# Expert groups of one 64-token and two 32-token experts in place of groups of four, in a fused attention and mixture-of-experts block

## The chip, the cores and the metric

The kernel runs on one core of one Trainium2 chip. The metric is device time in microseconds (us) of one execution. In the texts PE is TensorE, DVE is VectorE, ACT is ScalarE, POOL is GpSimd and SP is SyncE, whose queue issues nearly all transfers.

## The reference, cut to what matters

The block has one layer: RMS norm, one input projection, two groups of attention heads, an output projection into the residual stream, RMS norm, and a mixture of experts. There are 512 tokens of 1024 features. The change lies in the last part:

```python
pg = softmax(hf @ wg + bg); gsel = argmax(pg)                 # one of 4 expert groups per token
le = (hf @ we + be).reshape(n, 4, 8)[gsel]                    # its 8 experts
p_top, e_loc = top_k(softmax(le), 2)                          # two experts per token
gate = pg_sel * p_top / sum(p_top)
ys = (silu(xb @ w1[e]) * (xb @ w3[e])) @ w2[e]                # for each of 32 experts, on its own tokens
out[token] += gate * ys                                       # w1, w3: 1024 x 512, w2: 512 x 1024, float32
```

The 32 experts together hold 192 MB (1 MB here is 2^20 bytes, the size of one tile), so the weights of each expert are six tiles of [128, 2048] float32, two halves h of w1, of w3 and of w2, and 192 tiles are loaded in all.

## The kernel before, in words

**Up to about 280 us** the kernel runs the projections and the attention, and then the router. It leaves `pr`, with the count and the running position of each token in each expert.

**Order of the experts.** `sort_experts` (L1078) and `name_experts` (L1089) bring the 32 experts into an order of *places*: the first FIXED = 4 places are the experts 0 to 3, whatever their counts, and the places behind are the other experts by falling count. So the weights of the fixed places can be loaded before the router is done, and those of the others only when `who_i`, the list of names, is written. For them SP reads the name into a register (`values_load`) and the transfer's address depends on it. The last 12 places (from SMALL = 20 on) get 32 slots for tokens, the others 64. Tokens beyond that are the business of `overflow` (L1329), a branch that isn't taken here but whose condition every engine reads; it lies in group PAUSE = 7.

**Groups.** The experts are worked off in 13 groups (L657): ten pairs of 64-slot experts, and three groups of four 32-slot experts, at the places 20, 24 and 28, as groups 2, 7 and 12. A group always fills the 128 columns of PE: the tokens of expert e stand in the columns `d["parts"][e]`, 64 or 32 wide, and the products of the experts of a group (L1222 for w1 and w3, L1278 for w2) go to different columns of PE, and to different partitions of one accumulator in PSUM. They are issued expert by expert within each step r.

**Work of one group**: `hidden` (L1225) goes through four parts, each of four steps r and of one tile per expert: w1h0, w1h1, w3h0, w3h1 (group 0: w1h0, w3h0, w1h1, w3h1). Behind each of the 16 steps it issues what the lists `during` (L1413) hold for that step: for the group before, the eight sums `combine` (L1317: two products, L1325 and L1326, and an addition on DVE, L1327), and for the group behind, the gathering of its tokens by products with a one-hot matrix (`quarter`, L1164, and `turn`). The one-hot matrix is one comparison on DVE (`match`, L914). Then `turn_hidden` turns the result (L1261), and `outputs` (L1288) does the products with w2, in two halves. The first `combine` writes the sums into the tile `ma`, once the weights in it aren't needed any more.

**The ring.** The weight tiles go into places that are listed in `slots` (L662) and are taken in turn by `ring_tile` (L669): 19 places the first time, 17 afterwards, as the two places of `ma` then hold the sums. A transfer waits on SP's queue until the last product that read the old tile in its place is done, and everything behind it on that queue waits too. The order of a group's loads is part by part, and within a part expert by expert (`load_parts`, L691). Loads of group 1 that don't depend on the sort (8 of 12 tiles) are issued ahead of group 0's work, by calls of `next(ahead)` (L990, L1051). At most eight loads are in flight at a time.

**Around the branch**: of group 8 only the first tile is requested ahead of the branch in group 7 (L1411), and the rest behind it, at step 7 of the hidden products (L1430).

Of the kernel before, what the change touches and what calls it, by code (L numbers as in the profile page):

```python
# [3 lines left out]

# [1 line left out]

# [5 lines left out]
F32 = mybir.dt.float32  # L12
F32R = mybir.dt.float32r
# [9 lines left out]
P = 128  # L23
SEQ = 512
D = 1024
NT = SEQ // P
# [1 line left out]
NE = 32  # L28
HID = 512
SLOTS = 64  # L30
FIXED = 4
SMALL = 20
EPS = 1e-6
BIG = 1e30
# [60 lines left out]
def tile_block(ctx: ExitStack, tc: tile.TileContext, a: dict, out: bass.AP):  # L95
# [550 lines left out]
    for i, (g, n, j) in enumerate(ORDER):  # L646
# [7 lines left out]
    NP = NE // 2  # L654


    groups = [(0, 2), (2, 2), (20, 4), (4, 2), (6, 2), (8, 2), (10, 2), (24, 4), (12, 2), (14, 2), (16, 2), (18, 2),  # L657
              (28, 4)]
    NG = len(groups)
    pools = {"w8": pool_w8, "q8": pool_q8, "mx": pool_mx}  # L660
    ring, both = [0], []
    slots = [("q8", tag, 2) for tag in ("bt", "qs", "kl", "kh")] + [("xs", "e0", 1), ("xs", "e1", 1)]  # L662
    slots += [("q8", tag, 2) for tag in ("qs", "kl", "kh")] + [("n", "n0", 1), ("n", "n1", 1)]
    slots += [("mx", "ma", 1), ("mx", "ma", 1), ("mx", "mb", 2)]
    slots += [("w8", tag, 2) for tag in ("w_h", "w_l", "w_h", "w_l")]
    slots += [("mx", "mb", 2)]
    slots[0] = ("q8", "bt", 1)

    def ring_tile():  # L669

        pool, tag, bufs = slots[ring[0] % len(slots)]
        ring[0] += 1
        if tag == "ma":
            if ring[0] > len(slots):
                return ring_tile()
            if not both:
                both.append(pools[pool].tile([P, 2, 2048], F32, tag=tag, name=tag, bufs=bufs))
                return both[0][:, 0]
            return both[0][:, 1]
        return pools[pool].tile([P, 2048], F32, tag=tag, name=tag, bufs=bufs)  # L680
# [9 lines left out]

    def load_parts(i):  # L691
        last = i == NG - 1
        first, n_exp = groups[i]
        if first < FIXED:
            who = [first + e for e in range(n_exp)]
        else:
            who = [nc.values_load(place_id[0][0:1, first + e:first + e + 1], engines=[mybir.EngineType.SP],
                                  min_val=0, max_val=NE - 1) for e in range(n_exp)]
        t = {}
        for n, h in hidden_order(i) + [("w2", 0), ("w2", 1)]:  # L700
            src = {"w1": w1, "w3": w3, "w2": w2}[n]
            cuts = (0, 1024, 2048) if last and n + str(h) in ("w31", "w20") else (0, 2048)
            if last and n + str(h) == "w21":
                cuts = (0, 1024, 1536, 2048)
            for c, m in zip(cuts, cuts[1:]):
                for e in range(n_exp):
                    if (i, n, h, e) == (0, "w2", 1, 1):
                        continue
                    if c == 0:
                        t[n, h, e] = ring_tile()  # L710
                    dst, part = t[n, h, e], expert(who[e], h)(src)
                    if first >= FIXED:
                        part = part.rearrange("o p f -> p (o f)")
                    nc.sync.dma_start(dst[:, c:m], part[:, c:m])
                    if m == 2048:
                        yield t
        yield t
# [6 lines left out]

    place_id = []
    loads, ahead = load_parts(0), load_parts(1)


    x_tile = []
# [181 lines left out]
        ts_ = slice(t, t + 2)  # L911
        nc.vector.scalar_tensor_tensor(rank[:, ts_], pr[:, ts_], 1.0, act[:, ts_], op0=ALU.add, op1=ALU.mult)

    def match(oh, rk, ts_):  # L914
        n = ts_.stop - ts_.start
        m, w = oh.shape[2:]
        nc.vector.tensor_tensor(oh[:, ts_], rk[:, ts_].unsqueeze(3).to_broadcast([P, n, m, w]),
                                iota_s[:, :w].unsqueeze(1).unsqueeze(1).to_broadcast([P, n, m, w]), op=ALU.is_equal)

    def gather_part(px, oh, h, ts_):  # L920

        for t in ts_:
            x2 = x_tile[0][:, t, h * 512:(h + 1) * 512].rearrange("p (r b) -> p r b", r=4)
            one = oh[:, t].rearrange("p e s -> p (e s)").bitcast(F32)
            for r in range(4):
                nc.tensor.matmul(px[h][:, r], lhsT=x2[:, r], rhs=one, start=(t == NT - 1 and r == 0),
                                 stop=(t == 0 and r == 3), skip_group_check=True)
# [59 lines left out]
    next(loads), next(loads)  # L987
    while (1, 0) not in mixed:
        wv.step()
    next(ahead)  # L990
    wv.fill(3)
    xs = x_tile[0]
    while wv.step():
# [15 lines left out]
    entries = book[:, P:P + NT * 6 * NP].rearrange("p (t q c) -> p t q c", t=NT, q=NP)  # L1009
    pr = bank("o", (P, NT + 1, NE))  # L1010
    rank = small([P, NT, NE], "rank")
    oh0 = pools["n"].tile([P, NT, 2, SLOTS], F32R, tag="oh", name="oh", bufs=1)
    def half_match(n, t):
        for _ in range(n):
            yield
        place(t)
        match(oh0, rank[:, :, 0:2], slice(t, t + 2))

    def gates_first():
        for _ in range(10):  # L1020
# [26 lines left out]
    for s in range(NT):  # L1047
        nc.tensor.matmul(pr[:, NT], lhsT=ones_b, rhs=act[:, s], start=(s == 0), stop=(s == NT - 1))
    gather_part(px, oh0, 1, (2,))
    for _ in range(7):  # L1050
        next(ahead)  # L1051
    run(half_match(0, 0))
    nc.vector.reduce_sum(gs, ge, axis=AX.X)
# [67 lines left out]
    def wk(tag, shape, dt=F32, bufs=1):  # L1121
        return work.tile(list(shape), dt, tag=tag, name=tag, bufs=bufs)

    def one_hot(rk, second=False):
        n = rk.shape[-1]
        shape = [P, NT, n, P // n]
        if second:
            oh = wk("oht", shape, F32R, bufs=2)
        else:
            oh = pools["n"].tile(shape, F32R, tag="oh", name="oh", bufs=1)  # L1130
        match(oh, rk, slice(0, NT))
        return oh

    def dispatch(oh, p, px=None):

        ohs = [oh[:, t].rearrange("p e s -> p (e s)") for t in range(NT)]
        n_exp, w_exp = oh.shape[2:]
        rows = [slice(w_exp * e, w_exp * e + w_exp) for e in range(n_exp)]  # L1140
        d = {"px": px, "parts": rows}

        spare = not isinstance(p, int)

        def gather(h, ts_=tuple(reversed(range(NT)))):
            if not d["px"]:
# [40 lines left out]
        def finish(tag="mm"):  # L1187
            pbs = [bank(tag, (P, 2, 2, P)) for _ in range(2)]
            for t in range(NT):
                pb = pbs[t // 2][:, t % 2]  # L1190
                if not spare:
                    both = bass.AP(tensor=book.tensor, offset=book.offset,
                                   ap=[book.ap[0], [P + t * 6 * NP, 2], [1, P]])
                    nc.tensor.matmul(pb, lhsT=ohs[t], rhs=both, start=True, stop=True)
                else:
                    nc.tensor.matmul(pb[:, 0], lhsT=ohs[t], rhs=book[:, :P], start=True, stop=True)
                    nc.tensor.matmul(pb[:, 1, :6], lhsT=ohs[t], rhs=p[:, t], start=True, stop=True)
                yield
            oht = wk("st", [P, NT, P], F32R) if spare else wk("oht", [P, NT, P], F32R, bufs=2)
            own, bufs = ("x", 1) if spare else ("", 2)  # L1200
            gsl = pools["n"].tile([P, 1], F32, tag="gsl" + own, name="gsl", bufs=bufs)
            rsl = pools["n"].tile([P, 1], F32, tag="rsl" + own, name="rsl", bufs=bufs)
            m = 3 * n_exp
            g4 = pools["n"].tile([P, NT, 12], F32, tag="g4" + own, name="g4", bufs=bufs)
            c = 0 if spare else 6 * p
            for u, pb in enumerate(pbs):
                nc.scalar.copy(oht[:, 2 * u:2 * u + 2], pb[:, :, 0])
                nc.vector.tensor_copy(g4[:, 2 * u:2 * u + 2, :m], pb[:, :, 1, c:c + m])
            for e, part in enumerate(rows):
                x = 6 * (e // 2) + 2 * (e % 2)  # L1210
# [118 lines left out]
    def overflow():  # L1329
# [12 lines left out]
        with tc.If(rounds > 0):  # L1342
            move(rank_s[:, :, SMALL:], SLOTS // 2)
            with tc.For_i(0, rounds, 1):
                move(rank_s, -SLOTS)
                with tc.For_i(0, NP, 1) as iv:
# [5 lines left out]
                    dd = dispatch(one_hot(rk), own)  # L1352
# [27 lines left out]
            move(rank_s[:, :, SMALL:], -SLOTS // 2)  # L1380

    def group_dispatch(i, oh=None, px=None):
        first, n = groups[i]
        if oh is None:
            oh = one_hot((rank if first < FIXED else rank_s)[:, :, first:first + n], i == 1)
        return dispatch(oh, first // 2, px)

    d = group_dispatch(0, oh0, px)
    d["gather"](0, (1, 0))
# [15 lines left out]
    for i in range(NG):  # L1405
# [2 lines left out]
            rounds = nc.values_load(cint[0:1, 0:1], min_val=0, max_val=7)  # L1408
        if not last:
            rest = ahead if i == 0 else load_parts(i + 1)  # L1410
            for nxt in islice(rest, 1) if i == PAUSE else rest:  # L1411
                pass
        during, after = [[] for _ in range(16)], [[] for _ in range(8)]  # L1413
        if i == 0:
            def first_gather(d=d):
                d["gather"](1, (1, 0))
                d["take"](1)

            during[1] = [name_experts]
            during[3] = [turn_places]  # L1420
            during[4] = [first_gather]
            during[7] = [sort_places, partial(begin, 1)]
            during[11] = [lambda d=d: run(d["finish"]("o"))]
        else:
            for n in range(8):
                at_ = (3 if n < 4 else 7) if last else 3 + n // 2 if i == PAUSE else 4 + n // 2 * 2
                during[at_].append(partial(combine, *prev, n // 4, (n % 4,), i == 1))
        if not last:
            if i == PAUSE:
# [116 lines left out]
```

## Time and profile before

| | us |
|---|---|
| median of 3 runs (752.1 to 754.06) | 753.59 |
| the profiled execution | 753.97 |
| its span, from the first to the last instruction | 752.3 |
| PE busy | 726.8 (97%) |
| DVE busy | 389.1 (52%) |
| ACT busy | 302.2 (40%) |
| moved by DMA | 228.86 MB, mean 304 GB/s |

The page shows the span in 40 equal slices, so one slice is 18.8 us, and each digit is a busy share in tenths. A busy PE is not a PE at its peak, since products of several column ranges run at once and their ends are modelled. A row of a timeline gives the start and the length in us, the engine and the line, what is written and read, and in brackets the idle time before it with what ended it. A product of float32 leaves two records.

### The profile page before, as it was taken

What the parts mean: (1) busy time and instruction counts of PE and PEld (TensorE: products, weight loads), DVE (VectorE), ACT (ScalarE), POOL (GpSimd) and SP (SyncE); (2) the same over time, 40 slices, a digit from 0 to 9 for tenths busy, and PEclk for the clock granted to TensorE, in tenths of its full rate; (3) what the DMA queues carried; (4) which work ended last, traced back from release to release, by engine and by line L of the source; (5) the groups of instructions that cost most, each with busy time, mean ns of one, the idle gap of its engine ahead of it and who ended that gap; (6) DMA issues with size and microseconds to landing.
All of it is one profiled execution on the core that took longest, in us unless ns stands there. A gap on an engine that the chain in (4) does not pass through costs nothing. (4 is left out here: it accounts for less than half of the span.)

```text
span 752.3 us, 13147 instructions
## 1 busy us (share of the span) xinstructions
PE 726.8 (97%) x4812; PEld 454.7 (60%) x4812; DVE 389.1 (52%) x919; ACT 302.2 (40%) x708; POOL 91.7 (12%) x175
## 2 busy tenths in 40 slices
PE   9999999999999999999999999999779999999986
PEld 9899988887989984554435444453233444535324
DVE  4577778776665462254444554443433544444413
ACT  6665776876755340232232323221222232232100
POOL 0302100466665020000000000000000000000000
PEclk9999999999999999999999999999998999999999
DMA  8432121322573986649999999999999999999998
GB/s 314 134 127 86 54 84 57 113 58 64 166 313 112 368 362 253 240 194 381 418 419 421 421 420 422 421 421 421 416 421 419 423 419 421 422 419 420 418 409 298
DMA packets 46638, 228.86 MB, mean 304 GB/s; under 512 B 6724, under 2 KB 9412, under 8 KB 23656
## 3 DMA queue, kind: packets, MB, share of 16 engines
q1 hardware_dynamic: 46152, 227.83, 76.3%
q8 instruction: 40, 0.66, 0.3%
q14 instruction: 30, 0.25, 0.1%
q10 hardware_dynamic: 416, 0.14, 0.1%
HBM read 225.83 MB, written 2.11 MB: 303 GB/s over the span
## 5 line engine op out<-in xcount | busy, mean ns | idle before, releaser
L1156 ACT CAST part<-xs 128x256 fp32r<-128x256 f32 x176 | 63.1, 406 | 146.6 <-PE ps_mm L1164 60.1
L1157 DVE TENSOR_TENSOR part<-xs,part 128x256 fp32r<-128x256 f32 x176 | 66.6, 419 | 58.7 <-ACT part L1156 58.7
L1327 DVE TENSOR_TENSOR sums<-ps_o,sums 128x512 f32<-128x512 f32 x88 | 56.7, 686 | 71.0 <-PE ps_o L1326 71.0
L313 PE MATMUL ps_mm<-w_h,hTl 128*128 128x256 f32 x240 | 69.3, 289 | 0.1
L1222 PE MATMUL ps_mm<-qs,xt 128*64 128x512 f32 (+1 forms) x136 | 67.8, 610 | 0.0
L313 PE MATMUL ps_mm<-w_h,hTh 128*128 128x256 f32 x240 | 67.3, 281 | 0.0
L313 PE MATMUL ps_mm<-w_l,hTh 128*128 128x256 f32 x240 | 67.3, 280 | 0.0
L1222 PE MATMUL ps_mm<-mb,xt 128*64 128x512 f32 (+1 forms) x120 | 59.0, 610 | 4.1 <-PEq L1342 4.1
L1222 PE MATMUL ps_mm<-kl,xt 128*64 128x512 f32 (+1 forms) x120 | 59.3, 610 | 0.0
L1222 PE MATMUL ps_mm<-w_l,xt 128*64 128x512 f32 (+1 forms) x128 | 50.7, 602 | 0.0
L1222 PE MATMUL ps_mm<-kh,xt 128*64 128x512 f32 (+1 forms) x104 | 50.4, 600 | 0.0
L1222 PE MATMUL ps_mm<-w_h,xt 128*64 128x512 f32 (+1 forms) x120 | 46.8, 601 | 0.0
L313 PEld LDWEIGHTS ps_mm<-w_h,hTl 128*128 128x128 f32 x240 | 45.3, 189 | 0.6 <-DVE qn L438 0.3
L313 PEld LDWEIGHTS ps_mm<-w_l,hTh 128*128 128x128 f32 x240 | 45.3, 189 | 0.1
L313 PEld LDWEIGHTS ps_mm<-w_h,hTh 128*128 128x128 f32 x240 | 45.2, 188 | 0.0
L180 DVE TENSOR_TENSOR w_l<-w_raw,w_h 128x512 fp32r<-128x512 f32 x64 | 44.2, 707 | 1.0 <-ACT w_h L177 0.6
L1325 PE MATMUL ps_o<-yl,oht 128*128 128x512 f32 x96 | 43.2, 450 | 0.6 <-DVE sums L1327 0.6
L518 DVE TENSOR_TENSOR_SCAN p<-p,ones_f 128x513 f32<-128x513 f32 (+3 forms) x32 | 27.5, 858 | 30.5 <-POOL p L513 30.5
L1325 PEld LDWEIGHTS ps_o<-yl,oht 128*128 128x128 f32 x96 | 17.9, 187 | 41.8 <-issue 18.8
L1164 PEld LDWEIGHTS ps_mm<-part,oh 128*128 128x128 f32 x160 | 21.8, 191 | 33.3 <-DVE part L1157 20.3
L1251 DVE SCALAR_TENSOR_TENSOR sl<-ps_mm,rsl,sl 128x256 f32<-128x256 f32 x26 | 11.4, 479 | 58.6 <-PE ps_mm L1222 58.4
L1271 ACT ACTIVATE yh<-ps_sc,gsl 128x512 fp32r<-128x512 f32 (+2 forms) x29 | 18.5, 643 | 55.2 <-PE ps_sc L1278 55.2
(295 smaller groups left out, 1786.5 us busy)
## 6 DMA issues: line engine op xcount, KB each, us to landing
qs<-in_w SPq DMA_DIRECT2D x22, 1024.0 KB, 19.7
e<-in_w SPq DMA_DIRECT2D x22, 1024.0 KB, 19.8
kl<-in_w SPq DMA_DIRECT2D x21, 1024.0 KB, 19.7
kh<-in_w SPq DMA_DIRECT2D x21, 1024.0 KB, 19.7
n<-in_w SPq DMA_DIRECT2D x20, 1024.0 KB, 19.8
mb<-in_w SPq DMA_DIRECT2D x20, 1024.0 KB, 19.8
w_h<-in_w SPq DMA_DIRECT2D x20, 1024.0 KB, 19.8
w_l<-in_w SPq DMA_DIRECT2D x20, 1024.0 KB, 19.7
```

What stands on the lines that cost most here:

```text
L180: eng.tensor_tensor(part(wl, n), raw[i, n], part(wh, n).bitcast(F32), op=ALU.subtract)
L313: nc.tensor.matmul(pb[:, u], lhsT=x(t0 + u, k), rhs=y[:, k], start=first, stop=last, skip_group_check=True)
L518: nc.vector.tensor_tensor_scan(rev, rev, ones_f[:, 0:1].to_broadcast([P, n + 1]), 1.0, op0=ALU.mult, op1=ALU.mult)
L1156: nc.scalar.copy(hi, whole)
L1157: nc.vector.tensor_tensor(lo, whole, hi.bitcast(F32), op=ALU.subtract)
L1164: nc.tensor.matmul(d["rows"][:, q * 256:q * 256 + 256], lhsT=ohs[t], rhs=d[n][:, m], start=(n % 8 == 0 and m == 1), stop=(n % 8 == 7 and m ...
L1222: nc.tensor.matmul(ph[n][part], lhsT=d["xt"][h][:, r, part], rhs=w, start=(h == 0 and r == 0), stop=(h == 1 and r == 3))
L1251: nc.vector.scalar_tensor_tensor(s, ph["w3"][:, c], d["rsl"], s, op0=ALU.mult, op1=ALU.mult)
L1271: nc.scalar.activation(yh, py, AF.Copy, scale=gsl)
L1325: nc.tensor.matmul(pc, lhsT=oht[:, t], rhs=yl[:, c], start=True, stop=False)
L1327: nc.vector.tensor_tensor(sums[0][:, t, cs], pc, (xs if first else sums[0])[:, t, cs], op=ALU.add)
```

## The change

The groups are listed one by one: seven pairs, and six groups of one 64-slot expert and two 32-slot experts, in the order pair, three, pair, three, pair, three, pair, three, pair, three, pair, pair, three. Each place stands with its width, so a group's column ranges can differ in width. FIXED falls from 4 to 3; group 1 holds the fixed expert 2 and the places 20 and 21. Group 1 loads its six fixed tiles first, ahead of group 0's work, and the other twelve when the names are written, at step 1 of group 0. `slots` keeps its first round nearly as it was and then goes on in the order in which the groups give their places back. The one-hot matrix of a three takes two comparisons, one per width, and the copies of the gates two per half instead of one. In group 1 the sums of group 0 move from the steps 4, 6, 8 and 10 (two each) to the steps 8 to 15 (one each), since both places of `ma` now hold tiles of w1.

```diff
-FIXED = 4
+FIXED = 3
...
-    groups = [(0, 2), (2, 2), (20, 4), (4, 2), (6, 2), (8, 2), (10, 2), (24, 4), (12, 2), (14, 2), (16, 2), (18, 2),
-              (28, 4)]
+    pair = lambda p: [(p, SLOTS), (p + 1, SLOTS)]
+    three = lambda p, q: [(p, SLOTS), (q, SLOTS // 2), (q + 1, SLOTS // 2)]
+    groups = [pair(0), three(2, 20), pair(4), three(3, 22), pair(6), three(16, 24), pair(8), three(17, 26), pair(10),
+              three(18, 28), pair(12), pair(14), three(19, 30)]
...
-    slots = [("q8", tag, 2) for tag in ("bt", "qs", "kl", "kh")] + [("xs", "e0", 1), ("xs", "e1", 1)]
-    slots += [("q8", tag, 2) for tag in ("qs", "kl", "kh")] + [("n", "n0", 1), ("n", "n1", 1)]
-    slots += [("mx", "ma", 1), ("mx", "ma", 1), ("mx", "mb", 2)]
-    slots += [("w8", tag, 2) for tag in ("w_h", "w_l", "w_h", "w_l")]
-    slots += [("mx", "mb", 2)]
-    slots[0] = ("q8", "bt", 1)
+    q8 = lambda *tags: [("q8", tag, 1 if tag == "bt" else 2) for tag in tags]
+    early = q8("bt", "qs", "kl", "kh") + [("xs", "e0", 1), ("xs", "e1", 1)] + q8("qs", "kl", "kh")
+    early += [("n", "n0", 1), ("n", "n1", 1)]
+    w_h, w_l, mb, ma = ("w8", "w_h", 2), ("w8", "w_l", 2), ("mx", "mb", 2), ("mx", "ma", 1)
+    slots = early + [ma, ma, w_h, w_l, w_h, w_l, mb, mb] + early[:10]
+    again = [early[10], mb, mb] + early[0:2] + [w_h] + early[2:4] + [w_l] + early[4:6] + [w_h] + early[6:8] + [w_l]
+    again += early[8:10]
...
+        order = hidden_order(i) + [("w2", 0), ("w2", 1)]
+        fixed = [e for e, (place, _) in enumerate(groups[i]) if place < FIXED] if i == 1 else []
+        for e in fixed:
+            for n, h in order:
+                load(n, h, e, 0, 2048)
+                yield t
+        for e in range(len(groups[i])) if i == 1 else ():
+            if e not in fixed:
+                who[e] = nc.values_load(place_id[0][0:1, groups[i][e][0]:groups[i][e][0] + 1],
+                                        engines=[mybir.EngineType.SP], min_val=0, max_val=NE - 1)
...
-    for _ in range(7):
+    for _ in range(5):
         next(ahead)
...
+        c = 0
+        for rk, w in parts:
+            n = rk.shape[-1] * w
+            match(oh[:, :, c:c + n], rk, slice(0, NT), w)
+            c += n
...
+        rows, c = [], 0
+        for _, w in places:
+            rows.append(slice(c, c + w))
+            c += w
+        twos = sorted({e // 2 for e, _ in places})
...
-                nc.vector.tensor_copy(g4[:, 2 * u:2 * u + 2, :m], pb[:, :, 1, c:c + m])
+                for m, c in enumerate(twos):
+                    nc.vector.tensor_copy(g4[:, 2 * u:2 * u + 2, 6 * m:6 * m + 6], pb[:, :, 1, 6 * c:6 * c + 6])
...
-            for nxt in islice(rest, 1) if i == PAUSE else rest:
+            nxt = second[0] if i == 0 else next(rest)
+            for _ in () if i in (0, PAUSE) else rest:
                 pass
...
-            during[1] = [name_experts]
+            during[1] = [name_experts, lambda: list(ahead)]
...
-                at_ = (3 if n < 4 else 7) if last else 3 + n // 2 if i == PAUSE else 4 + n // 2 * 2
+                at_ = (3 if n < 4 else 7) if last else 8 + n if i == 1 else 3 + n // 2 if i == PAUSE else 4 + n // 2 * 2
```

## Rows read from the trace of the kernel before

**Rows 1.** The page, busy tenths in 40 slices.
```profile
PE   9999999999999999999999999999779999999986
...
DMA  8432121322573986649999999999999999999998
```
**Rows 2.** Stretches: start:end, length, each engine's busy us (records), PEclk, DMA share, GB/s.
```profile
326.00:336.00 10.00, 10.00 (x49) 5.06 (x50) 4.67 (x10) 3.46 (x9) 0.00 (x0) 1.00 0.08 31
336.00:344.00 8.00, 8.00 (x40) 3.99 (x41) 3.24 (x6) 1.30 (x3) 0.00 (x0) 1.00 0.80 283
344.00:740.00 396.00, 381.84 (x2080) 165.81 (x2080) 173.98 (x413) 105.91 (x272) 0.00 (x0) 0.99 1.01 419
```
**Rows 3.** Timeline of SP's queue: issues of loads.
```profile
270.30 0.38 SPq L714 DMA_DIRECT2D mb<-in_w  x1
...
318.05 4.84 SPq L714 DMA_DIRECT2D n<-in_w  x2
335.01 0.33 SPq L714 DMA_DIRECT2D mb<-in_w  x1
```
**Rows 4.** Timeline of PE in the hidden products of group 1.
```profile
322.36 1.03 PE L1222 MATMUL ps_mm<-ma,xt 128*64 128x512 f32 x4
...
327.45 0.59 PE L1222 MATMUL ps_mm<-mb,xt 128*64 128x512 f32 x1
327.45 0.59 PE L1222 MATMUL ps_mm<-w_h,xt 128*64 128x512 f32 x1
327.88 0.59 PE L1222 MATMUL ps_mm<-mb,xt 128*64 128x512 f32 x1
...
328.40 0.50 PE L1325 MATMUL ps_o<-yl,oht 128*128 128x512 f32 x1
...
329.44 0.64 PE L1164 MATMUL ps_sc<-part,oh 128*128 128x256 f32 x4
...
334.82 0.59 PE L1222 MATMUL ps_mm<-w_l,xt 128*64 128x512 f32 x1
...
341.76 0.59 PE L1222 MATMUL ps_mm<-w_l,xt 128*64 128x512 f32 x1
```
**Rows 5.** Timeline of PE: first transposes behind the hidden products of a group.
```profile
346.02 0.39 PE L1261 MATMUL ps_mm<-ident,sl 128*128 128x128 f32 x2
...
379.20 0.44 PE L1261 MATMUL ps_mm<-ident,sl 128*128 128x128 f32 x2
...
412.42 0.40 PE L1261 MATMUL ps_mm<-ident,sl 128*128 128x128 f32 x2
...
552.58 0.38 PE L1261 MATMUL ps_mm<-ident,sl 128*128 128x128 f32 x2
...
595.81 0.40 PE L1261 MATMUL ps_mm<-ident,sl 128*128 128x128 f32 x2
```
**Rows 6.** Timeline of PE from group 1 (64 wide) to group 2 (32 wide).
```profile
355.01 0.59 PE L1278 MATMUL ps_sc<-kl,sl 128*64 128x512 f32 x1
...
355.54 0.62 PE L1222 MATMUL ps_mm<-e,xt 128*32 128x512 f32 x2
...
355.99 0.60 PE L1222 MATMUL ps_mm<-e,xt 128*32 128x512 f32 x2
```
**Rows 7.** The same stretch, PE's weight loads.
```profile
354.58 0.14 PEld L1278 LDWEIGHTS ps_sc<-kl,sl 128*64 128x64 f32 x1
...
355.54 0.11 PEld L1222 LDWEIGHTS ps_mm<-e,xt 128*32 128x32 f32 x2 [0.81 <-issue]
```
**Rows 8.** Timeline of DVE: the names are written, and group 1's comparison.
```profile
284.53 0.18 DVE L1094 CAST who_i<-ps_o 1x32 int32<-1x32 f32 x1 [0.94 <-PE ps_o L1093]
...
295.80 0.69 DVE L917 TENSOR_TENSOR oht<-rank,iota_s 128x512 fp32r<-128x512 f32 x1
```
**Rows 9.** Timeline of PE: the wait at the branch in group 7.
```profile
535.78 0.72 PE L1222 MATMUL ps_mm<-mb,xt 128*32 128x512 f32 x1 [4.15 <-PEq L1342]
```
**Rows 10.** The chain that ended last: start, us, what.
```profile
729.55 10.29 DMA qs<-in_w
...
748.08 0.42 DVE sums L1480
```

More of the change, by code (lines that the diff above doesn't have):

```diff
@@ L2 @@
 from functools import partial
-from itertools import islice
 import numpy as np
@@ L661, in tile_block @@
     ring, both = [0], []
-    slots = [("q8", tag, 2) for tag in ("bt", "qs", "kl", "kh")] + [("xs", "e0", 1), ("xs", "e1", 1)]
-    slots += [("q8", tag, 2) for tag in ("qs", "kl", "kh")] + [("n", "n0", 1), ("n", "n1", 1)]
-    slots += [("mx", "ma", 1), ("mx", "ma", 1), ("mx", "mb", 2)]
-    slots += [("w8", tag, 2) for tag in ("w_h", "w_l", "w_h", "w_l")]
-    slots += [("mx", "mb", 2)]
-    slots[0] = ("q8", "bt", 1)
+    q8 = lambda *tags: [("q8", tag, 1 if tag == "bt" else 2) for tag in tags]
[5 more added lines that the diff above has]
+    again += early[8:10]
     def ring_tile():
-        pool, tag, bufs = slots[ring[0] % len(slots)]
+        while ring[0] >= len(slots):
+            slots.extend(again)
+        pool, tag, bufs = slots[ring[0]]
         ring[0] += 1
         if tag == "ma":
-            if ring[0] > len(slots):
-                return ring_tile()
             if not both:
@@ L692, in load_parts, with load @@
         last = i == NG - 1
[L693 to L701, printed above, removed]
+        who, t = {}, {}
+        def load(n, h, e, c, m):
+            place = groups[i][e][0]
+            if place >= FIXED and e not in who:
+                who[e] = nc.values_load(place_id[0][0:1, place:place + 1], engines=[mybir.EngineType.SP], min_val=0,
+                                        max_val=NE - 1)
+            if c == 0:
+                t[n, h, e] = ring_tile()
+            part = expert(who.get(e, place), h)({"w1": w1, "w3": w3, "w2": w2}[n])
+            if place >= FIXED:
+                part = part.rearrange("o p f -> p (o f)")
+            nc.sync.dma_start(t[n, h, e][:, c:m], part[:, c:m])
+        order = hidden_order(i) + [("w2", 0), ("w2", 1)]
[8 more added lines that the diff above has]
+                                        engines=[mybir.EngineType.SP], min_val=0, max_val=NE - 1)
+        for n, h in order:
             cuts = (0, 1024, 2048) if last and n + str(h) in ("w31", "w20") else (0, 2048)
@@ L705, in load_parts @@
             for c, m in zip(cuts, cuts[1:]):
-                for e in range(n_exp):
-                    if (i, n, h, e) == (0, "w2", 1, 1):
+                for e in range(len(groups[i])):
+                    if (i, n, h, e) == (0, "w2", 1, 1) or e in fixed:
                         continue
[L709 to L714, printed above, removed]
+                    load(n, h, e, c, m)
                     if m == 2048:
@@ L726, in tile_block @@
     loads, ahead = load_parts(0), load_parts(1)
+    second = []
     x_tile = []
@@ L912, in place, with match @@
         nc.vector.scalar_tensor_tensor(rank[:, ts_], pr[:, ts_], 1.0, act[:, ts_], op0=ALU.add, op1=ALU.mult)
-    def match(oh, rk, ts_):
-        n = ts_.stop - ts_.start
-        m, w = oh.shape[2:]
+    def match(oh, rk, ts_, w):
+        n, m = ts_.stop - ts_.start, rk.shape[-1]
+        oh = oh.rearrange("p t (m w) -> p t m w", w=w)
         nc.vector.tensor_tensor(oh[:, ts_], rk[:, ts_].unsqueeze(3).to_broadcast([P, n, m, w]),
@@ L923, in gather_part @@
             x2 = x_tile[0][:, t, h * 512:(h + 1) * 512].rearrange("p (r b) -> p r b", r=4)
-            one = oh[:, t].rearrange("p e s -> p (e s)").bitcast(F32)
+            one = oh[:, t].bitcast(F32)
             for r in range(4):
@@ L989, in tile_block @@
         wv.step()
-    next(ahead)
+    second.append(next(ahead))
     wv.fill(3)
@@ L1011, in tile_block @@
     rank = small([P, NT, NE], "rank")
-    oh0 = pools["n"].tile([P, NT, 2, SLOTS], F32R, tag="oh", name="oh", bufs=1)
+    oh0 = pools["n"].tile([P, NT, P], F32R, tag="oh", name="oh", bufs=1)
     def half_match(n, t):
@@ L1016, in half_match @@
         place(t)
-        match(oh0, rank[:, :, 0:2], slice(t, t + 2))
+        match(oh0, rank[:, :, 0:2], slice(t, t + 2), SLOTS)
     def gates_first():
@@ L1122, in wk, with one_hot @@
         return work.tile(list(shape), dt, tag=tag, name=tag, bufs=bufs)
-    def one_hot(rk, second=False):
-        n = rk.shape[-1]
-        shape = [P, NT, n, P // n]
+    def one_hot(parts, second=False):
         if second:
-            oh = wk("oht", shape, F32R, bufs=2)
+            oh = wk("oht", [P, NT, P], F32R, bufs=2)
         else:
-            oh = pools["n"].tile(shape, F32R, tag="oh", name="oh", bufs=1)
-        match(oh, rk, slice(0, NT))
+            oh = pools["n"].tile([P, NT, P], F32R, tag="oh", name="oh", bufs=1)
+        c = 0
[3 more added lines that the diff above has]
+            c += n
         return oh
     def dispatch(oh, p, px=None):
-        ohs = [oh[:, t].rearrange("p e s -> p (e s)") for t in range(NT)]
-        n_exp, w_exp = oh.shape[2:]
-        rows = [slice(w_exp * e, w_exp * e + w_exp) for e in range(n_exp)]
+        ohs = [oh[:, t] for t in range(NT)]
+        spare = not isinstance(p, list)
+        places = [(e, SLOTS) for e in range(2)] if spare else p
+        rows, c = [], 0
[3 more added lines that the diff above has]
+        twos = sorted({e // 2 for e, _ in places})
         d = {"px": px, "parts": rows}
-        spare = not isinstance(p, int)
         def gather(h, ts_=tuple(reversed(range(NT)))):
@@ L1202, in finish @@
             rsl = pools["n"].tile([P, 1], F32, tag="rsl" + own, name="rsl", bufs=bufs)
-            m = 3 * n_exp
             g4 = pools["n"].tile([P, NT, 12], F32, tag="g4" + own, name="g4", bufs=bufs)
-            c = 0 if spare else 6 * p
             for u, pb in enumerate(pbs):
                 nc.scalar.copy(oht[:, 2 * u:2 * u + 2], pb[:, :, 0])
-                nc.vector.tensor_copy(g4[:, 2 * u:2 * u + 2, :m], pb[:, :, 1, c:c + m])
-            for e, part in enumerate(rows):
-                x = 6 * (e // 2) + 2 * (e % 2)
+                for m, c in enumerate(twos):
+                    nc.vector.tensor_copy(g4[:, 2 * u:2 * u + 2, 6 * m:6 * m + 6], pb[:, :, 1, 6 * c:6 * c + 6])
+            for (e, _), part in zip(places, rows):
+                x = 6 * twos.index(e // 2) + 2 * (e % 2)
                 nc.vector.reduce_sum(gsl[part], g4[part, :, x:x + 2], axis=AX.XY)
@@ L1351, in overflow @@
                                           min_val=0, max_val=NE - 1) for e in range(2)]
-                    dd = dispatch(one_hot(rk), own)
+                    dd = dispatch(one_hot([(rk, SLOTS)]), own)
                     run(dd["finish"]("o"))
@@ L1382, in group_dispatch @@
     def group_dispatch(i, oh=None, px=None):
-        first, n = groups[i]
+        g = groups[i]
         if oh is None:
-            oh = one_hot((rank if first < FIXED else rank_s)[:, :, first:first + n], i == 1)
-        return dispatch(oh, first // 2, px)
+            cuts = [(g[0][0], 2, SLOTS)] if len(g) == 2 else [(g[0][0], 1, SLOTS), (g[1][0], 2, SLOTS // 2)]
+            oh = one_hot([(rank_s[:, :, c:c + n], w) for c, n, w in cuts], i == 1)
+        return dispatch(oh, g, px)
     d = group_dispatch(0, oh0, px)
```

## The prediction

> **What bounds the kernel now.** I read the slices of the page first [rows 1]: TensorE (PE) is busy in nearly every slice, and from slice 19 to the end the 16 DMA engines are too. So the expert part has two limits that nearly meet. The rows by stretch [rows 2] price the second: from 344 to 740 us DMA is full at 419 GB/s, so one tile of 1 MB (1.049e6 bytes) costs 1.049/0.419 = 2.50 us. Before 344 there are holes: in 326–336 the share is 0.08, in 336–344 it is 0.80. Idle there is 10 x 0.92 + 8 x 0.20 = 9.2 + 1.6 = 10.8 us.
>
> Why the hole is there, the queue's issues show [rows 3]: after the two n loads (issued from 318.05) the next tile, mb, is issued only at 335.01. Its ring place holds half of w1 of group 1 (w1h1), and PE releases that when it goes on to w3 at 334.82 [rows 4]. The pair of group 1 gives its places back at pair speed while nothing else is free.
>
> PE's own speed is one period per group, whatever the group: the transposes after the hidden products come at 346.02, 379.20 and 412.42, 33.2 us apart [rows 5], with the outputs of a pair and the hidden products of a four between the first two, and the reverse between the others. DMA needs 12 x 2.50 = 30 us for a pair, 60 for a four. Only around group 7 is the interval longer: 552.58 to 595.81 is 43.2, so 10.1 us more. Two things lie in or just ahead of it: PE waits there for tiles, and the branch of the overflow check cost 4.15 us shortly before [rows 9].
>
> The end hangs on DMA: the chain of waits goes through a last load issued at 729.55 that lands at 739.84, and then through products and sums to 748.08 [rows 10]. So a microsecond by which DMA's unbroken stream starts earlier is one at the end, as long as PE can follow.
>
> **The change, part by part.** The profiled execution took 753.97 us (span 752.3), 0.38 above the median of the runs, 753.59.
>
> *Order and size of groups.* All 192 tiles are still loaded, so after DMA is full nothing is saved. What counts is the hole. Group 1 becomes expert 2 (6 tiles, loaded early) and two small experts (12 tiles). By the end of group 0 the same number of tiles has been issued as before (31, up to n), so DMA still runs dry at about 326 + 10 x 0.08 = 326.8. After that, places are listed as group 1 releases them: 2 after w1h0, 2 after w1h1, 3 after w3h0, then 3 and 3 and 3. On PE's clock of before [rows 4]: w1h0 ends at 327.45. From issue to data I take 1.25 us (mb issued at 335.01, the DMA share being that of one idle stretch up to 336). So data from 328.7: idle 1.9; two tiles, to 333.7. w1h1 ends at 334.82 before, with two pairs of sums of 1.04 us in it (328.40 to 329.44); these move to steps 8 to 15, so it ends at 332.7, data 334.0: idle 0.3, to 339.0. w3h0 takes 341.76 - 334.82 = 6.94 and has four single sums in place of two pairs, some 0.3 more for the added size changes: it ends at 339.9, data 341.2: idle 2.2; three tiles, to 348.7. The next three places come at about 346, so no more idle. Sum: 4.4 us idle instead of 10.8, a gain of 6.4.
>
> *Does DMA stay full?* Group 1 ends near 356 with DMA queued to 371, 15 us ahead. A pair on PE takes 33.1 and DMA 30, so a pair costs 3 us of that lead; a three needs 45 us of DMA and adds 12. With pairs and threes in turn the lead never reaches zero. The ring holds 17 tiles, so where the lead passes some 30 us PE waits for data in a three; that delays PE, not DMA.
>
> *Does PE follow?* Without its waits PE could reach the last group up to 10.1 us earlier [rows 5], DMA 6.4. So DMA still ends last, with under 4 us to spare: 0.6 us more PE time in each of six threes uses it up.
>
> *A step of a group of three.* Before, a step is 0.43 us, whether two 128x64 products run in it (327.45 to 327.88, mb and w_h, which start within 0.01) or four 128x32 ones [rows 4, 6]. A three would put one 64-wide and two 32-wide products side by side, on columns that don't overlap. No row shows that. Bounds: 0.43 (all at once, also nothing below, since one product alone streams for that long) and, if each size waits for the other, 0.43 + 0.43 and two size changes. A change costs 0.53 - 0.43 = 0.10 (355.01 to 355.54) and 0.02 in the step behind it (355.54 to 355.99, 0.45) [rows 6]: 0.12 each, 1.10 us for the step. I take 0.43, the rows nearest in kind being those of disjoint columns of one size, 64 or 32 wide, two or four of them.
>
> What speaks against it is in the weight loads [rows 7]: inside one size they go ahead of their products (354.58 for the product of 355.01), at the change to 32 they start with it, at 355.54. The Trainium skill, page "TensorEngine Tiling (Array Packing)", section "Key Properties", says that changing the tiling mode, not just the tile, drains TensorE. By that the sum would be the first rival's, and the trace agrees as far as it goes; but every change in it is between products that share columns, which would wait for each other anyhow.
>
> *Loads behind the sort.* Two tiles that were issued by 270.30 (mb) now wait for the experts' names, written at 284.53 [rows 8], and for two register loads on SP: I estimate an issue near 287. Behind them on SP's queue stand bt and the following loads of group 1, about 2 us later than their places allow. Hidden: their products start at 322.36 at the earliest, and DMA has work gaps until then. Without that cover a late tile would cost what it is late, at most 2 us. The register loads of the fixed expert vanish.
>
> *Smaller edits.* One comparison of 0.69 us [rows 8] becomes two of half the width per three: between 0 and 0.69 us more on DVE; in group 1 PE's gather waits for it, so up to 0.7 us, and I take 0.15. The copies of gates are two for one, on a DVE that is half idle. In group 1 the last sum comes after the last hidden product, ahead of the gating on DVE: at most one addition, 0.7 us on PE, hidden by the DMA lead. The branch now falls into a three, with 12 tiles behind it in place of 16; eight loads in flight (20 us) cover its 4.15 us [rows 9], else up to 4. The last three keeps its cuts and the number of steps after the last landing: no change there.
>
> Sum: 753.6 - 6.4 = 747.2 us.
>
> **Rivals.**
> 1. *Sizes exclude each other* (slower). Where: every step of the six threes, 48 steps each (24 products of two records). Price: 48 x (1.10 - 0.43) = 32 us per three, 193 in all. Off it come PE's 10 us of slack and the waits for the last tiles, for which I allow 8 of the 10.29 us of the last load [rows 10]: about 753.6 + 175 = 929. If the two records of a product stay together, two changes per product fall away (24 x 0.24 x 6 = 35 us): 894. For: weight loads that start only with the products at each size change. Against: those changes share columns. It decides from 0.6 us per three on.
> 2. *Products overlap, but weights aren't loaded ahead.* Then only the 0.12 at each size change is paid, twice per step (11.5 us per three) or twice per product (5.8): 35 to 69 in all, less the 10 of slack: 779 to 813. For and against: the same weight loads; where the steps are of one size, nothing is lost at all.
> 3. *The gain is given back.* The stream starts earlier but runs dry at the branch (up to 4 us), or PE's additions of under a microsecond per three take the rest: 750 to 755. For: PE has under 4 us to spare. Against: eight loads in flight at 535.
>
> **How the numbers follow.** Forecast 0.50, rival 1 0.31, rival 2 0.10, rival 3 0.09. The likeliest gives 747.2; its own range is 741 (if the issue latency between releases hides, nearly all of 10.8 is gained) to 751.4. About 0.3% (2.3 us) is what a measurement of this kernel can tell from no change: faster is below 751.3. Faster 0.51 (the forecast and a little of rival 3), same 0.09, slower 0.40. With rival 1 at 0.31 the range has to reach into it: 740 to 925, which leaves out its upper part (0.10) and gains over 13 us (0.03).
>
> **What would show it.** Right: DMA idle between 326 and 344 falls from 10.8 to some 4 us; in group 1 one 64-wide and two 32-wide products start within 0.03 us of each other and the next step 0.43 later; the period stays 33.1 in pairs and threes; the last landing moves from 739.8 to about 733. Wrong: 32-wide products that start only when the 64-wide one is through and a period of 60 us or more in threes (rival 1); steps of 0.5 to 0.7 (rival 2); a DMA share below 1 around 535 (rival 3).

## The result, and the profile after

| | before | after |
|---|---|---|
| median of the runs (four each) | 753.83 us (752.1 to 754.24) | 884.79 us (884.03 to 885.67) |
| ratio to before, 95% interval | | 1.1747 (1.1728 to 1.1765) |
| span of the profiled execution | 752.3 us | 882.4 us |
| PE busy | 726.8 us (97%) | 869.5 us (99%) |

The kernel became 131 us slower. The forecast was 747.2; the first rival, sizes that exclude each other, is what happened, and its lower variant (894) is 9 us off.

The page after, slices of PE and DMA as in [rows 1]:

```profile
span 882.4 us, 13119 instructions
...
PE   9999999999999999999999999999999999999998
...
DMA  7432213139294966799789978898789978898603
```

DMA was full from slice 19 on before; now its share goes up and down with the groups and is full nowhere for long. PE has lost even the two sevens. The stretches of [rows 2], with the same columns, say the same:

```profile
326.00:336.00 10.00, 10.00 (x37) 2.55 (x36) 1.52 (x4) 1.91 (x5) 0.00 (x0) 1.00 0.50 188
336.00:344.00 8.00, 8.00 (x34) 2.85 (x32) 2.19 (x5) 2.26 (x6) 0.00 (x0) 1.00 0.49 174
344.00:740.00 396.00, 394.38 (x1564) 136.04 (x1562) 138.58 (x341) 82.85 (x215) 0.00 (x0) 1.00 0.85 337
```

PE is busy for all of it, but finishes 1564 records in 396 us where it finished 2080; over the whole execution the two kernels have about as many (4788 and 4812). So the engine is slower at its own work; the granted clock is 1.00 (2.4 GHz), no lower than before. The start of group 1 on PE shows how, first the products, then the weight loads (PEld) of the same products. What LDWEIGHTS loads here are the tokens in `xt`; the experts' tiles are streamed past them.

```profile
323.28 1.07 PE L1244 MATMUL ps_mm<-ma,xt 128*64 128x512 f32 x2
324.28 1.05 PE L1244 MATMUL ps_mm<-mb,xt 128*32 128x512 f32 x4
325.26 1.07 PE L1244 MATMUL ps_mm<-ma,xt 128*64 128x512 f32 x2
326.27 1.05 PE L1244 MATMUL ps_mm<-mb,xt 128*32 128x512 f32 x4
```

```profile
323.28 0.19 PEld L1244 LDWEIGHTS ps_mm<-ma,xt 128*64 128x64 f32 x2
324.28 0.14 PEld L1244 LDWEIGHTS ps_mm<-mb,xt 128*32 128x32 f32 x4 [0.81 <-issue]
325.26 0.19 PEld L1244 LDWEIGHTS ps_mm<-ma,xt 128*64 128x64 f32 x2 [0.84 <-issue]
326.27 0.14 PEld L1244 LDWEIGHTS ps_mm<-mb,xt 128*32 128x32 f32 x4 [0.81 <-issue]
```

x2 and x4 are the two records of each float32 product: the two 32-wide experts run together, the 64-wide one runs alone, and the columns they use don't overlap. One round of the three products takes 325.26 - 323.28 = 1.98 us. All at once it would be 2 x 0.43 = 0.86, one size after the other 1.72; the remaining 0.26, put down to the two changes of size, are 0.13 each. The weights of the next size are loaded only when its products start, as at the one change in [rows 7].

The first transposes behind the hidden products of a group, as in [rows 5]:

```profile
363.06 0.41 PE L1283 MATMUL ps_mm<-ident,sl 128*128 128x128 f32 x2 [0.59 <-DVE sl L1273]
...
404.83 0.39 PE L1283 MATMUL ps_mm<-ident,sl 128*128 128x128 f32 x2
...
454.83 0.39 PE L1283 MATMUL ps_mm<-ident,sl 128*128 128x128 f32 x2
```

The first interval (outputs of a three, hidden products of a pair) is 41.8 us, the second (outputs of a pair, hidden products of a three) 50.0; before, each was 33.2. A three costs 8.6 + 16.8 = 25.4 us more than 24 products (16 hidden, 8 output) at 0.43 per record would, so 1.06 per product. It is less than 1.98 - 0.86 = 1.12, probably since between some products stands other work, 128 wide, where the size changes anyway. Six threes make 6 x 25.4 = 152 us; 131 reached the end, because waits of PE went away. Most of them lay around the branch. Before, not one but two intervals were longer there: in front of the one that [rows 5] end with stands another, from

```profile
511.64 0.39 PE L1261 MATMUL ps_mm<-ident,sl 128*128 128x128 f32 x2
```

to 552.58, 40.9 us. With the 43.2 behind it that is 17.9 us more than two intervals of 33.1. After, only the interval with the branch is longer than its like:

```profile
588.40 0.40 PE L1283 MATMUL ps_mm<-ident,sl 128*128 128x128 f32 x2
...
640.05 0.38 PE L1283 MATMUL ps_mm<-ident,sl 128*128 128x128 f32 x2
```

That is 51.7 us instead of 50.0, so some 16 of the 17.9 are gone; most of the rest is in the last group, where PE waited for tiles before. The chain that ended last holds no transfer any more:

```profile
PE 29%; DVE 0%; issue 0%; ACT 0%; DVEq 0%
```

And the wait at the branch, 4.15 us in [rows 9], is now

```profile
616.92 1.04 PE L1244 MATMUL ps_mm<-e,xt 128*64 128x512 f32 x2 [0.34 <-PEq L1364]
```

### The profile page after: what moved, and what is told of

Read it like the earlier page. It is cut to its first block, busy times and chain, and to the rows that moved or that the text cites. A ratio compares the mean times of both kernels' runs of the same rounds, so it can differ in the third digit from the quotient of the medians.

```text
span 882.4 us, 13119 instructions
## 1 busy us (share of the span) xinstructions
PE 869.5 (99%) x4788; PEld 467.0 (53%) x4788; DVE 390.7 (44%) x937; ACT 302.2 (34%) x708; POOL 91.8 (10%) x175
## 5 line engine op out<-in xcount | busy, mean ns | idle before, releaser
L1244 PE MATMUL ps_mm<-kl,xt 128*64 128x512 f32 (+1 forms) x128 | 65.6, 607 | 0.0
L1244 PE MATMUL ps_mm<-w_l,xt 128*64 128x512 f32 (+1 forms) x112 | 57.8, 608 | 0.0
L1244 PE MATMUL ps_mm<-qs,xt 128*64 128x512 f32 (+1 forms) x112 | 57.5, 606 | 0.0
L1244 PE MATMUL ps_mm<-kh,xt 128*64 128x512 f32 (+1 forms) x112 | 56.2, 604 | 0.0
L1244 PE MATMUL ps_mm<-w_h,xt 128*64 128x512 f32 (+1 forms) x104 | 53.5, 607 | 0.0
L1244 PE MATMUL ps_mm<-mb,xt 128*64 128x512 f32 (+1 forms) x144 | 51.9, 605 | 0.0
L1294 DVE SCALAR_TENSOR_TENSOR yl<-ps_sc,gsl,yh 128x512 fp32r<-128x512 f32 (+2 forms) x29 | 20.1, 695 | 67.0 <-ACT yh L1293 63.5
L1244 PE MATMUL ps_mm<-n,xt 128*64 128x512 f32 (+1 forms) x104 | 48.7, 607 | 0.0
L1293 ACT ACTIVATE yh<-ps_sc,gsl 128x512 fp32r<-128x512 f32 (+2 forms) x29 | 18.5, 643 | 86.1 <-PE ps_sc L1300 86.1
L1287 ACT COPY sl<-ps_mm 128x256 f32<-128x256 f32 x26 | 10.1, 387 | 102.3 <-PE ps_mm L1283 102.3
```

The costliest lines, as they stand in the source:

```text
L1244: nc.tensor.matmul(ph[n][part], lhsT=d["xt"][h][:, r, part], rhs=w, start=(h == 0 and r == 0), stop=(h == 1 and r == 3))
L1293: nc.scalar.activation(yh, py, AF.Copy, scale=gsl)
L1294: nc.vector.scalar_tensor_tensor(yl, py, gsl, yh.bitcast(F32), op0=ALU.mult, op1=ALU.subtract)
```

## Experiments

Seven kernels ran. Theory W (width): products of different width don't run at the same time, whatever their columns, and that is the whole loss. Its rivals: the number of products side by side (N for three or four), and other parts of the change (ring, order, gathering).

**1. The change, with one width in the threes.** The 64-slot expert's product is issued as two 32-wide ones with the same weight tile, in the products with w2 too; groups, ring and loads stay.

```diff
+        d["cols"] = [(e, c) for e, part in enumerate(rows)
+                     for c in (cut(part, 32) if len(rows) == 3 else [part])]
...
-                for e in range(len(d["parts"])):
-                    hidden_product(ph, d, n, h, r, e, t[n, h, e][:, r * HID:(r + 1) * HID])
+                for e, part in d["cols"]:
+                    hidden_product(ph, d, n, h, r, part, t[n, h, e][:, r * HID:(r + 1) * HID])
```

> The changed kernel, but in groups of three the 64-slot expert is multiplied as two products of 32 columns with the same weights, so that every product of a three is 128x32. Theory W (products of different width exclude each other): the step falls back to 0.43 us with four products in it, the period of a three to 33.1 us, and what is left of the change is the hole in DMA: about 747 us (743 to 752). Rival N (the order of loads, the ring or the place of the branch cost the time, or a three as such): the time stays near 885. Rival P (each product beyond two per step costs): over 800.

Measured: 748.32 us (before beside it: 752.72), ratio 0.994 (0.9921 to 0.9959). More instructions, 136.5 us less than the change. PE at the start of group 1:

```profile
322.05 0.62 PE L1246 MATMUL ps_mm<-ma,xt 128*32 128x512 f32 x2
322.06 0.62 PE L1246 MATMUL ps_mm<-mb,xt 128*32 128x512 f32 x2
322.50 0.60 PE L1246 MATMUL ps_mm<-ma,xt 128*32 128x512 f32 x2
```

Four products start within 0.01 us, the next four 0.45 later. So the loss is the mix of widths, and neither the number of products nor the rest of the change: theory W stands. What is left is the kernel that the forecast had in mind, and its stretches (columns as above) test the rest of it:

```profile
326.00:336.00 10.00, 10.00 (x77) 4.13 (x70) 3.65 (x8) 2.98 (x8) 0.00 (x0) 1.00 0.93 348
336.00:344.00 8.00, 8.00 (x54) 2.61 (x53) 3.17 (x5) 0.58 (x1) 0.00 (x0) 1.00 0.86 326
344.00:732.00 388.00, 377.34 (x2296) 163.13 (x2288) 174.36 (x428) 105.83 (x272) 0.00 (x0) 0.99 1.01 419
```

DMA is idle for 10 x 0.07 + 8 x 0.14 = 1.8 us where it was 10.8, and full from there to its end. The chain that ended last hangs on DMA again:

```profile
691.50 19.73 DMA kh<-in_w
711.35 11.32 DMA bt<-in_w
722.79 10.06 DMA w_l<-in_w
```

The last landing is at 722.79 + 10.06 = 732.85; it was 739.84 [rows 10]. This version is faster than both kernels, than the one before by 4.4 us (3.1 to 5.9).

**2. Mixed width without the change.** The kernel before, with the second expert of each of its ten pairs as two 32-wide products, so 64, 32, 32 side by side (the list `cols` as above, cut for `e == 1` of pairs).

> The kernel before, groups, loads and ring untouched; only in its ten pairs the second expert is multiplied as two products of 32 columns, so that a step has the widths 64, 32, 32. Theory W: 24 x 1.13 us = 27 us more per pair, as in the threes of the changed kernel (323.28 to 325.26 is 1.98 us per product instead of 0.86), 271 us in all, less the same 31 us of slack that the six threes left uncharged (6 x 27 = 162, measured 131): about 994 us (960 to 1025). Rival N: 754, since loads and groups are those of before.

Measured: 987.54 us, ratio 1.3113 (1.3076 to 1.315). PE shows the change's rhythm in a kernel that has nothing else of it:

```profile
358.35 1.07 PE L1223 MATMUL ps_mm<-mb,xt 128*64 128x512 f32 x2
359.35 1.05 PE L1223 MATMUL ps_mm<-w_h,xt 128*32 128x512 f32 x4
360.33 1.07 PE L1223 MATMUL ps_mm<-mb,xt 128*64 128x512 f32 x2
361.33 1.05 PE L1223 MATMUL ps_mm<-w_h,xt 128*32 128x512 f32 x4
```

1.98 us for a round here too. Ten pairs lose 987.5 - 752.7 = 235 us, 23.5 each. So the loss needs neither threes nor the changed ring.

**3. The control.** Both experts of each pair as two 32-wide products: four products, one width.

```diff
-                     for c in (cut(part, 32) if e == 1 and len(rows) == 2 and not spare else [part])]
+                     for c in (cut(part, 32) if len(rows) == 2 and not spare else [part])]
```

> The kernel before, with both experts of each pair multiplied as two products of 32 columns: four products of one width per step. Control for the mix in pairs: as many products and more. Theory W: no change, 754 us (751 to 757). Rival P (each product beyond two per step costs): slower by at least half of what the mix in pairs costs, over 860.

Measured: 754.06 us, ratio 1.0014 (1.0001 to 1.0027). Twice the instructions in the pairs cost at most 0.3%. Nothing is wrong with a product cut in two; it is the neighbour of another width.

**4. By width.** The change, with the products of a part in the threes issued by width: the four steps of the wide expert, then those of the two narrow ones; the products with w2 too. The 128-wide work that belongs to the four steps comes behind them.

```diff
+                for es in ((0,), (1, 2)):
+                    for r in range(4):
+                        for e in es:
+                            hidden_product(ph, d, n, h, r, e, t[n, h, e][:, r * HID:(r + 1) * HID])
+                for _ in range(4):
+                    for f in next(between, ()):
+                        f()
```

> The changed kernel, but in threes the products of one tile part are issued by width: four steps of the 64-slot expert, then the same four of the two others, so that the width changes twice per four products instead of twice per product; what stands between the steps comes behind the four. Theory W in two parts: exclusion alone costs 24 x 0.855 = 20.5 us per three and stays, the changes (0.99 - 0.855 = 0.13 each) fall from 48 to 12 per three, 4.8 us less per three, 29 in all: about 856 us (845 to 866). If the cost were one of the changes alone (1.13 us per product as two changes of 0.57), three quarters of 27 us would go: about 763. Rival N: 885.

Measured: 880.93 us, ratio 1.1693 (1.1666 to 1.172). A miss: 3.9 us less than the change, where 29 were expected. The products do what was worked out:

```profile
322.42 3.60 PE L1244 MATMUL ps_mm<-ma,xt 128*64 128x512 f32 x8
325.95 3.63 PE L1244 MATMUL ps_mm<-mb,xt 128*32 128x512 f32 x16
329.51 0.74 PE L1187 MATMUL ps_mm<-part,oh 128*128 128x256 f32 x4
330.96 0.39 PE L1187 MATMUL ps_mm<-part,oh 128*128 128x256 f32 x1 [0.72 <-DVE part L1180]
```

The eight records of the wide product alone take 325.95 - 322.42 = 3.53 us, 0.44 each, and the sixteen of the two narrow ones as long, since two run at a time. A part takes 329.51 - 322.42 = 7.1 us (four rounds of the change: 7.9). But behind it the gathering, now in one bunch, waits for DVE (0.72 in the last row). And in the branch's group PE waits for a tile:

```profile
582.18 0.40 PE L1292 MATMUL ps_mm<-ident,sl 128*128 128x128 f32 x2
...
615.31 5.52 PE L1244 MATMUL ps_mm<-e,xt 128*64 128x512 f32 x8 [5.65 <-DMA e<-in_w]
...
644.85 0.38 PE L1292 MATMUL ps_mm<-ident,sl 128*128 128x128 f32 x2
```

From transposes to transposes that is 62.7 us, 11 more than the 51.7 of the change. Nor can this run tell why the sizes exclude each other.

**5. By width, spread.** The same, with the other work behind every second step.

```diff
+                        if r % 2:
+                            for f in next(between, ()):
+                                f()
-                for _ in range(4):
-                    for f in next(between, ()):
-                        f()
```

> As the order by width (880.9 us), but the work of other groups that belongs to the four steps of a part is put behind every second step, not all of it behind the part. Theory B (the 25 us that the order by width fell short of its forecast are waits of the bunched work): one part of a three still takes 7.1 us of products, DVE and ACT have time between, the waits of the bunched work (0.7 us each) fall away and the intervals of threes come down from 41.1 to 39.5 and from 47.8 to about 45.5: 856 to 868 us. Theory E (the bunching isn't it: a product of one width costs as much whether the other comes next or not): 877 to 886 us.

Measured: 870.27 us, ratio 1.155 (1.1524 to 1.1575): between the two theories, 2 us from B and 7 from E. Transposes of three groups that follow each other, and those around the branch's group:

```profile
405.44 0.39 PE L1292 MATMUL ps_mm<-ident,sl 128*128 128x128 f32 x2
...
453.05 0.39 PE L1292 MATMUL ps_mm<-ident,sl 128*128 128x128 f32 x2
...
494.12 0.40 PE L1292 MATMUL ps_mm<-ident,sl 128*128 128x128 f32 x2
...
582.81 0.39 PE L1292 MATMUL ps_mm<-ident,sl 128*128 128x128 f32 x2
...
636.23 0.38 PE L1292 MATMUL ps_mm<-ident,sl 128*128 128x128 f32 x2
```

The branch's group takes 53.4 us, 9.3 less than with the bunch: that accounts for most of the 10.7 us won (11.5 if each time is taken against the kernel before that ran beside it, 752.72 us for experiments 1 to 4 and 753.59 for 5 to 7). So the bunch did cost something, but at the branch, not in every three: 47.6 and 41.1 us are the intervals of experiment 4 (47.8 and 41.1) and not the 45.5 and 39.5 of theory B. Two intervals are 3.1 us shorter than in the change (91.8), where the expectation of experiment 4 counted 4.8, from 36 changes of size fewer per three, and theory B 6.8 (39.5 + 45.5 = 85.0). An account after the fact: the other work is 128 wide, so every place where it stands is a change too (0.52 us instead of 0.43 from 327.88 to 328.40 in [rows 4]), and fewer changes fall away than were counted. It wasn't tried by itself. With it the 25 us that experiment 4 fell short are 11 at the branch, some 6 x 1.8 = 11 in changes that stayed, and a few us open.

**6. The ring's order undone.** Experiment 1, with the ring's places in one fixed cycle.

```diff
-    slots = early + [ma, ma, w_h, w_l, w_h, w_l, mb, mb] + early[:10]
-    again = [early[10], mb, mb] + early[0:2] + [w_h] + early[2:4] + [w_l] + early[4:6] + [w_h] + early[6:8] + [w_l]
-    again += early[8:10]
+    slots = early + [ma, ma, w_h, w_l, w_h, w_l, mb, mb]
+    again = early + [w_h, w_l, w_h, w_l, mb, mb]
```

> The kernel with all products of the threes 32 wide (748.3 us, DMA idle 1.8 us between 326 and 344), with one thing undone: from the second round on, the ring places are taken in one fixed cycle (w_h, w_l, w_h, w_l, mb, mb behind the eleven early ones) and not in the order in which group 1 gives them back. Theory R (the order of release is what closes the hole): the next tile after the 31st waits for a place of w3h0, given back at about 339, and the next three for places that come at 346 to 355; DMA is idle for some 20 us between 327 and 355 and the time is 748 + 19 = 767 us (758 to 775). Theory L (the early loads and the fixed expert close it, the listing does nothing): at most 5 us idle there and 748 to 751 us.

Measured: 767.64 us, ratio 1.019 (1.0167 to 1.0213). SP's queue and the stretches:

```profile
319.27 4.84 SPq L708 DMA_DIRECT2D n<-in_w  x2
341.24 0.34 SPq L708 DMA_DIRECT2D w_h<-in_w  x1
347.88 0.33 SPq L708 DMA_DIRECT2D w_l<-in_w  x1
354.32 0.33 SPq L708 DMA_DIRECT2D w_h<-in_w  x1
```

```profile
326.00:344.00 18.00, 18.00 (x134) 6.88 (x126) 6.89 (x16) 4.75 (x12) 0.00 (x0) 1.00 0.21 76
344.00:360.00 16.00, 15.41 (x118) 5.67 (x110) 8.87 (x24) 4.46 (x12) 0.00 (x0) 1.00 0.46 167
360.00:740.00 380.00, 360.71 (x2089) 156.72 (x2090) 165.19 (x401) 99.95 (x257) 0.00 (x0) 0.99 1.01 419
```

One tile per 6.4 to 6.6 us goes out while free places stand behind the one that SP waits for: bt, which experiment 1 filled again at 331.18, is filled at 360.97 here. Idle: 18 x 0.79 + 16 x 0.54 = 22.9 us, 21.1 more than in experiment 1, and 19.3 us at the end (18.5, each against its own kernel before). Theory R holds.

**7. A pair as second group.** Experiment 1 with the groups pair, pair, three, pair, ..., FIXED = 4 and the ring's cycle of before. The early loads of group 1's fixed expert and the new steps of group 0's sums are undone with it; the branch, still in a three, falls into group 8.

```diff
-    groups = [pair(0), three(2, 20), pair(4), three(3, 22), pair(6), three(16, 24), pair(8), three(17, 26), pair(10),
-              three(18, 28), pair(12), pair(14), three(19, 30)]
+    groups = [pair(0), pair(2), three(4, 20), pair(6), three(5, 22), pair(8), three(16, 24), pair(10), three(17, 26),
+              pair(12), three(18, 28), pair(14), three(19, 30)]
```

> The kernel with all products of the threes 32 wide, with a pair of fixed experts as group 1 again (threes as groups 2, 4, 6, 8, 10 and 12; four fixed places; ring places in the cycle of the kernel before, which is the release order of a pair; the sums of group 0 at their old steps). Theory H (the gain of 4 to 5 us comes from the hole, and a three as the second group is what closes it): DMA is idle for 9 to 11 us between 326 and 344, and the last landing and the time are 7 to 9 us later than with a three there: 755 us (752.5 to 758). Theory A (pairs and threes in turn are what helps, in the evenness of PE's and DMA's demands, wherever the first one stands): the hole is there but the time stays at 747 to 750 us.

Measured: 755.03 us, ratio 1.0019 (1.0001 to 1.0036); experiment 1 had 0.994. The hole is back:

```profile
326.00:336.00 10.00, 10.00 (x49) 5.01 (x48) 4.67 (x10) 3.42 (x9) 0.00 (x0) 1.00 0.09 22
336.00:344.00 8.00, 8.00 (x41) 3.79 (x41) 3.25 (x6) 1.30 (x3) 0.00 (x0) 1.00 0.80 300
```

10.7 us idle, 8.9 more than in experiment 1 and 6.7 at the end (5.8, each against its own kernel before). Theory H holds: pairs and threes in turn bring no gain by themselves; a three as second group does, with its early loads and its ring order. These were undone together here; experiment 6 shows that without the ring order a three as second group loses instead.

## Why the prediction was wrong

**The step that failed** is "A step of a group of three ... I take 0.43", with the bounds 0.43 and 1.10. Both rows it was taken from are of one width, and the value was chosen by nearness in kind (columns that don't overlap). But the rows differed from the step in question in the one thing that counts. Measured: 1.98 us per product of two records, 0.99 per step, near the upper bound. Of that, 0.86 are the streams one after the other (experiment 4: 0.44 for a wide record by itself) and 0.13 one change of size, where the bound counted two at 0.12. The prediction had the sign in its hands: the weight load that starts only with its product at the change of size [rows 7]. It was set aside because the products there share columns. The change and experiments 1 to 3 show that this was no reason. The Trainium skill, page "TensorEngine Tiling (Array Packing)", section "Key Properties", says that a change of the tiling mode, not just of the tile, drains TensorE. The trace agrees in the effect: 1.98 us where sizes differ, 0.86 where they don't. Whether it is a drain in that sense or two sizes that can't be resident together, no run here tells.

**The rivals.** Rival 1 is right in place and mechanism, and in its variant with both records of a product together: 26.4 us per three worked out, 25.4 measured. It came out 9 us too high. Six of them are the price, 1.0 too much in each of six threes; the other three are the net of smaller terms, the largest of which is PE's slack at the branch, where the prediction saw one longer interval (10.1 us) instead of two (17.9). By the prediction's own argument, "under 4 us to spare" was too little for the same reason: 17.9 - 6.4 is 11.5. The sign given for rival 1, a period of 60 us or more in threes, did not come and did not fit its price: a third of the products of a three lie in the next interval, so that the loss shows as 50.0 and 41.8. Rival 2 (overlap, only the weights late) asked for 0.12 per change and is refuted by the 64-wide product that runs alone. Rival 3 could not show in the change; in experiment 1 DMA did not run dry at the branch. The chances, 0.51 for faster against 0.31 for rival 1, leaned the wrong way.

**The rest of the sum**, tested in experiment 1, has the mechanism right, and its total comes close in part by luck. The hole: 4.4 us idle forecast, 1.8 measured, since mb went out at 325.69, not at 327.45; group 1's products began 2 us earlier (320.38 instead of 322.36), and the forecast had kept the old clock. DMA stayed full from 344 on at 419 GB/s. Time: 747.2 forecast, 748.32 measured. But 9.0 us less idle brought 4.4 us (3.1 to 5.9), where the forecast had 6.4 for 6.4: the hole closed further than forecast and paid less than one for one, and the two errors offset each other. Why it paid less is open. The last landing (733 forecast, 732.85 measured) is that of an execution of 746.35 us, the fastest of six. Loads behind the sort: issue near 287 estimated; in the change 284.61, without a wait on PE:

```profile
284.61 0.90 SPq L709 DMA_DIRECT2D mb<-in_w  x2
```

The branch fell into a three with 4.40 us of waiting in experiment 1, and DMA stayed full over it. PE waits for tiles in a three, as forecast for a lead over 30 us; in experiment 1:

```profile
627.74 1.04 PE L1302 MATMUL ps_sc<-n,sl 128*32 128x512 f32 x2 [0.83 <-DMA n<-in_w]
```

In the change itself the gain could not show: PE became the only bound, and SP's queue waits for it (us in total, times, longest; the same wait was 61.2 us in total before):

```profile
SPq L709 <- PE ps_mm L1244: 299.5, 64, 9.0
```

## What to carry to other kernels

In these runs (float32, 128 rows, widths 64 and 32, 512 columns streamed) products side by side in different columns of PE ran together only where they had one width; a narrower partner cost a full stream of its own and some 0.13 us per change. Other widths and types were not run. A wide product cut into several of the common width with the same weights was nearly free here (at most 0.3%), so cut it before mixing. When the only row that resembles a new situation shows a warning, and it is set aside by an argument, price the warning first: one run that mixes two widths would have shown the sign.

## What was not expected of the hardware

- Cutting ten pairs into four 32-wide products instead of two 64-wide ones adds as many instructions again and moves the time by 0.14% (0.01% to 0.27%).
- What a microsecond of early DMA idle time costs at the end is not settled here: by the medians 4.4 us for 9.0 (experiment 1 against before), 6.7 for 8.9 (experiment 7) and 19.3 for 21.1 (experiment 6). The idle times are those of one profiled execution each, and executions of one kernel differ by 3 to 4 us.
- Ring places in an order other than that of their release cost more than the hole of before was long: 19.3 us against 10.8, with places free behind the one that was waited for.
